# A transformer pair on one core: joined first group, norm factors by token first, weight pieces of one conversion

## Chip, cores and metric

One core of a Trainium2 chip. The metric is the device time of one execution in microseconds (us), the median over runs. One profiled execution by itself gives the views that are quoted here.

## What is computed

256 tokens of width 2048, all in float32, go through two blocks.

The first block: an rms norm, one projection `proj = rmsnorm(h) @ w_in + b_in` cut into q, k, v, gates and convolution inputs, an mLSTM of 4 heads, a short causal convolution, two branch projections merged by sigmoid gates and `w_out`; then a norm, `w_up`, a causal depthwise convolution, `silu(gate) * val`, `w_down`, and a last norm.

The second block has two layers, each `x = x + rms_norm(mixer(rms_norm(x)))`: a gated linear attention (GLA, chunks of 64, 4 heads) and a latent attention (MLA, 16 heads, low-rank queries and keys of width 512 that are normed, rotary halves, softmax, `silu` gates).

The norm that occurs everywhere is

```python
y = x * rsqrt(mean(x * x) + eps) * g
```

where the factor belongs to a token. The kernel multiplies by g before a projection and by the factor R after it.

## The kernel before, in words

Activations lie with features on the 128 partitions and the 256 tokens along the free dimension: `h` has 16 blocks of 128x256 (`KD` = 16). Every projection goes through `dense`. Float32 precision comes from a split of both operands into a high part (fp32r) and the rest: `split` (L425) makes the parts of an activation block with one ScalarE (ACT) and one VectorE (DVE) instruction (L434, L435), and `need` (L301) those of the weights (L312 on ACT, L313 on DVE). For each unit of 128 weight columns, `dense` issues a pair of matmuls: the high weights with 512 moving columns (L359) and the low weights with 256 (L360). The kind "B" (v, gv) has three matmuls with 344 columns (L372 to L374).

`plan` (L46) lists all projections as groups in the order of the run, cuts the stream of weight units into conversions of at most `SUB` = 1040 columns (`subs`, 721 of them), and joins two of these to a piece (`pieces`, 361). A piece is one transfer by SyncE's queue (SP, L299) into one of `RAW` = 3 raw buffers of 2 x 1040 columns. `wunit` (L320) asks for the conversion that is `st["look"]` = `LOOK` = 3 ahead of the one in use; there are `LOOK` + 1 = 4 buffers `hl` for converted pieces. A conversion waits for its transfer and for TensorE to finish with the buffer that it overwrites; a transfer waits for DVE's conversion of the raw buffer's old content.

An accumulator `acc` has two banks for two output blocks, and there are two of them. A group of four blocks takes both: it runs the first half of the input blocks for all four outputs, then the second half for the first two outputs, then for the last two. `evac` (L409) empties an accumulator with one ACT and one DVE instruction, at a priority raised by 150.

The scheduler orders each engine's instructions by priority, which is the order in the program unless raised, with a model of times; on the chip every engine then runs its queue in that order. `tc.issue_after(st["mm"])` keeps a side matmul behind the last matmul of a group.

The start (L538 to L573): nine junk matmuls, then transfers of x blocks (`xload`) and parts of the first pieces in turn, then all 16 splits with three conversions between them. The first norm: squares are summed into `st1` while the four qk groups run (L637 to L646); `mk_R1` (L578) runs after the third. `bc_sum` (L468) sums over features and spreads the sum to all partitions as a row of 256 tokens (R); `col_sum` (L474) puts it in a column with tokens on partitions (Rc), needed by v and gv. `rsqrt` (L463) is a square root on ACT and a reciprocal on DVE. The third norm (`mk_R3`, L866) needs the sums `s3` and `s4` before and after the first block's last norm, and makes Ro, R as rows and Rc as columns.

On GpSimd (POOL), `rope_tables` (L587) computes the rotary angles in one long run of instructions. The bias vb of v comes by three transfers on POOL's queue (L731); DVE adds it when it empties v (L735), first into `ifc`, which TensorE then transposes (L654). In GLA, `gkc` (L892) is the like of ifc; TensorE transposes it at L902.

`out_norm` (L481) runs an output projection and its norm; it lowers the look-ahead to 2 for the last two groups. After GLA, `x3` (L1047) forms the next input block by block: DVE scales y (L1052), POOL adds it to h (L1053), and `split` follows. MLA's low-rank inputs are emptied by `low_rank_in` (L1068); `low_rank_scale` (L1075) makes their row factors; `skc` is a column made from a row by two transposes (L1118 to L1123).

The functions that the change touches stand here:

## Time and profile before

| | |
|---|---|
| median of 3 runs | 2060.18 us (2059.97 to 2061.51) |
| the profiled execution by itself | 2059.47 us |
| its span, first to last instruction | 2057.8 us |
| TensorE matmul busy | 2005.0 us, 97% |
| VectorE busy | 1433.7 us, 70% |
| ScalarE busy | 1153.3 us, 56% |
| GpSimd busy | 392.9 us, 19% |
| DMA | 385.61 MB, mean 187 GB/s |

How to read it: an engine runs its instructions in order, so a stall is found where an instruction has idle time before it, and the releaser named behind it is the instruction that ended the wait. TensorE's idle time is 2057.8 - 2005.0 = 52.8 us in the whole span, the start before its first matmul and the end after its last among it.

### The profile page before, as it was taken

To read this page: it belongs to the slowest core of one execution; us is meant where nothing else is said; L and a number is where in the kernel's file an instruction comes from. 1 tells how busy PE (TensorE), PEld (TensorE's weight loads), DVE (VectorE), ACT (ScalarE), POOL (GpSimd) and SP (SyncE) were. 2 spreads that over 40 slices of the span, in tenths; PEclk is the share of its full clock that TensorE was granted. 3 is DMA by queue.
4 is the path that set the end of the run, shared out by engine and by line. 5 is a ranking of instruction groups with operands and counts; after the bars stand their busy time and mean duration, and the time that the engine had idled before them with its cause. 6 is when DMAs were issued, how large, how long until landed. Compare 5 with 4: busy or idle time off the path is not lost. (4 is left out here: it accounts for less than half of the span.)

```text
span 2057.8 us, 30674 instructions
## 1 busy us (share of the span) xinstructions
PE 2005.0 (97%) x12438; PEld 1849.7 (90%) x12438; DVE 1433.7 (70%) x1758; ACT 1153.3 (56%) x1599; POOL 392.9 (19%) x333
## 2 busy tenths in 40 slices
PE   8799999999999999999999999999999999999997
PEld 7788999999999999999999999989999988989996
DVE  7568776666667888864588876676767558777754
ACT  6454555555556666654466666655666556544453
POOL 8511000010122111100011113321220025112312
PEclk9999999999999999999999999999999999999998
DMA  7443555555555555555555555535545544554343
GB/s 289 155 164 144 204 200 204 191 204 204 205 201 188 205 204 198 198 200 206 203 205 203 197 195 206 205 120 198 180 171 188 201 170 178 194 188 145 109 165 112
DMA packets 55743, 385.61 MB, mean 187 GB/s; under 512 B 6384, under 2 KB 6640, under 8 KB 10544
## 3 DMA queue, kind: packets, MB, share of 16 engines
q1 hardware_dynamic: 55152, 382.91, 51.5%
q8 instruction: 97, 1.59, 0.3%
q0 software_dynamic: 304, 0.73, 0.1%
q14 instruction: 46, 0.38, 0.1%
q10 hardware_dynamic: 144, 0.01, 0.0%
HBM read 381.52 MB, written 2.10 MB: 186 GB/s over the span
## 5 line engine op out<-in xcount | busy, mean ns | idle before, releaser
L313 DVE TENSOR_TENSOR hl<-raw,hl 128x1024 fp32r<-128x1024 f32 (+3 forms) x722 | 941.0, 1311 | 353.3 <-ACT hl L312 352.8
L359 PE MATMUL acc<-xhl,hl 128*128 128x512 f32 x3440 | 1138.1, 384 | 9.5 <-DVE xhl L435 7.8
L312 ACT ACTIVATE hl<-raw 128x1024 fp32r<-128x1024 f32 (+3 forms) x722 | 756.8, 1052 | 395.3 <-PE acc L360 250.5
L360 PE MATMUL acc<-xhl,hl 128*128 128x256 f32 x3440 | 940.9, 274 | 1.6 <-DVE hl L313 1.6
L359 PEld LDWEIGHTS acc<-xhl,hl 128*128 128x128 f32 x3440 | 652.6, 190 | 105.0 <-DVE xhl L435 6.9
L360 PEld LDWEIGHTS acc<-xhl,hl 128*128 128x128 f32 x3440 | 662.7, 193 | 3.3 <-DVE hl L313 2.9
L359 PE MATMUL acc<-ghl,hl 128*128 128x512 f32 x688 | 225.4, 382 | 0.0
L412 ACT ACTIVATE t<-acc 128x512 f32<-128x512 f32 x138 | 82.2, 596 | 192.6 <-PE acc L360 171.8
L360 PE MATMUL acc<-ghl,hl 128*128 128x256 f32 x688 | 187.5, 273 | 0.0
L413 DVE TENSOR_TENSOR u<-acc,t 128x512 f32<-128x512 f32 x138 | 94.9, 688 | 104.3 <-ACT t L412 104.3
L418 POOL TENSOR_TENSOR uR<-u,R 128x512 f32<-128x512 f32 x51 | 69.8, 1369 | 443.3 <-DVE u L413 436.0
L359 PEld LDWEIGHTS acc<-ghl,hl 128*128 128x128 f32 x688 | 130.0, 189 | 18.1
L360 PEld LDWEIGHTS acc<-ghl,hl 128*128 128x128 f32 x688 | 132.1, 192 | 0.0
L456 POOL TENSOR_TENSOR ss<-ss,sq 128x512 f32<-128x512 f32 x41 | 64.9, 1584 | 223.0 <-ACT sq L451 213.6
L374 PE MATMUL acc<-hl,xhl 128*128 128x344 f32 x288 | 90.4, 314 | 1.5 <-DVE hl L313 1.5
L372 PE MATMUL acc<-hl,xhl 128*128 128x344 f32 x288 | 91.0, 316 | 0.0
L373 PE MATMUL acc<-hl,xhl 128*128 128x344 f32 x288 | 90.3, 313 | 0.0
L795 POOL TENSOR_TENSOR m<-u 128x256 f32<-128x256 f32 x16 | 24.9, 1553 | 336.1 <-DVE u L793 336.1
L783 PE MATMUL acc<-hmxc,hl 128*128 128x512 f32 x256 | 84.7, 382 | 0.0
L359 PE MATMUL acc<-mg,hl 128*128 128x512 f32 x256 | 83.9, 382 | 0.0
L831 ACT ACTIVATE cv<-uR,vec 128x256 f32<-128x256 f32 x86 | 46.9, 593 | 57.9 <-POOL uR L418 57.9
L359 PE MATMUL acc<-ohl,hl 128*128 128x512 f32 x224 | 73.7, 383 | 0.0
(515 smaller groups left out, 2490.2 us busy)
## 6 DMA issues: line engine op xcount, KB each, us to landing
raw<-stream SPq DMA_DIRECT2D x330, 1024.0 KB, 4.8
raw<-stream SPq DMA_DIRECT2D x21, 1032.0 KB, 4.8
raw<-stream SPq DMA_DIRECT2D x4, 512.0 KB, 7.2
out<-y SPq DMA_DIRECT2D x8, 256.0 KB, 2.1
h<-xT SPq DMA_DIRECT2D x7, 256.0 KB, 7.2
raw<-stream SPq DMA_DIRECT2D x1, 1028.0 KB, 4.7
raw<-stream SPq DMA_DIRECT2D x1, 1008.0 KB, 4.7
raw<-stream SPq DMA_DIRECT2D x1, 988.0 KB, 6.6
```

What stands on the lines that cost most here:

```text
L312: S.activation(hl[:, 0, x:y_], src, AF.Copy)
L313: V.tensor_tensor(hl[:, 1, x:y_], src, hl[:, 0, x:y_].bitcast(F32), op=ALU.subtract)
L359: PE.matmul(o, lhsT=wh, rhs=both(x), start=(k == 0), stop=False)
L360: mm = PE.matmul(o[:, T:2 * T], lhsT=wl, rhs=part(x, 0), start=False, stop=(k == nk - 1))
L372: PE.matmul(o, lhsT=xh, rhs=both(wh), start=(k == 0), stop=False)
L373: PE.matmul(o, lhsT=xl, rhs=both(wh), start=False, stop=False)
L374: mm = PE.matmul(o, lhsT=xh, rhs=both(wl), start=False, stop=(k == nk - 1))
L412: S.activation(halves(t[:, :nb]), out_of(ps[:, :nb, T:2 * T]), AF.Copy)
L413: V.tensor_tensor(halves(u[:, :nb]), out_of(ps[:, :nb, 0:T]), halves(t[:, :nb]), op=ALU.add)
L418: (eng or V).tensor_tensor(w[:, :nb], u[:, :nb], bc2(R)[:, :nb], op=ALU.mult)
L456: (eng or G).tensor_tensor(self.ss, self.ss, sq, op=ALU.add)
L783: PE.matmul(o, lhsT=wh, rhs=both(x), start=(k == 0), stop=False)
```

## The change

`plan` joins the first two qk groups to one group of four blocks, and a piece is now one conversion. There are four raw buffers of 1040 columns and five converted buffers. The start transfers fewer x blocks ahead of the first pieces, and the splits are made as `dense` asks for them, four blocks ahead (`lazy`). The first norm's factors are made after the fourth qk group; all factors but the second norm's and the heads' are made as columns by token (`col_sum`, `second`) and turned into rows by `to_row`: a diagonal matrix from the column and the identity, and a matmul with ones. The joined group's evacuations, and those of cq, lose the raised priority. vb is transferred by SyncE's queue.

```diff
--- before.py
+++ after.py
@@ -61,7 +61,8 @@
         g.append(dict(name=name, kind=kind, blocks=blocks, k0=k0, nk=nk, n=nk * n, order=order))
 
     W = "w_in"
-    for h in range(4):
+    add("qk", "A", [(W, _blk(o + h * P)) for h in range(2) for o in (0, 512)], 0, KD)
+    for h in (2, 3):
         add("qk", "A", [(W, _blk(h * P)), (W, _blk(512 + h * P))], 0, KD)
     vcols = np.concatenate([_blk(3072, 8), _blk(1024, 1024)])
     for c in range(3):
@@ -128,8 +129,7 @@
         pos += e["n"]
     subs.append(cur)
     pieces, at = [], 0
-    for i in range(0, len(subs), 2):
-        n = sum(subs[i:i + 2])
+    for n in subs:
         pieces.append((at, n))
         at += n
     return g, subs, pieces, at
@@ -247,7 +247,7 @@
     from contextlib import ExitStack
     es = ExitStack()
     pool = lambda **k: es.enter_context(tc.tile_pool(**k))
-    RAW, LOOK, WARM = 3, 3, 9
+    RAW, LOOK, WARM = 4, 4, 9
     cst = pool(name="cst", bufs=1)
     rawp = pool(name="rawp", bufs=RAW)
     hlp = pool(name="hlp", bufs=LOOK + 1)
@@ -287,10 +287,10 @@
     def emit_dma(upto):
         while st["dma"] <= min(upto, len(pieces) - 1):
             p = st["dma"]
-            r = rawp.tile([P, 2 * SUB], F32, tag="raw", name="raw")
+            r = rawp.tile([P, SUB], F32, tag="raw", name="raw")
             raws[p] = r
             st["dma"] += 1
-            if p > 1:
+            if p > 3:
                 piece_dma(p, 0, pieces[p][1])
 
     def piece_dma(p, x, y_):
@@ -301,19 +301,16 @@
     def need(q_):
         while st["sub"] <= min(q_, len(subs) - 1):
             q = st["sub"]
-            p, half = divmod(q, 2)
-            emit_dma(p + RAW - 1)
+            emit_dma(q + RAW - 1)
             n = subs[q]
-            o = subs[q - 1] if half else 0
             hl = hlp.tile([P, 2, SUB], F32R, tag="hl", name="hl")
-            cuts = (0, n) if q else (0, n // 2, n)
+            cuts = (0, n) if q else (0, n // 4, n // 2, n)
             for x, y_ in zip(cuts, cuts[1:]):
-                src = raws[p][:, o + x:o + y_]
+                src = raws[q][:, x:y_]
                 S.activation(hl[:, 0, x:y_], src, AF.Copy)
                 V.tensor_tensor(hl[:, 1, x:y_], src, hl[:, 0, x:y_].bitcast(F32), op=ALU.subtract)
             hls[q] = hl
-            if half == 1:
-                raws.pop(p, None)
+            raws.pop(q, None)
             hls.pop(q - 8, None)
             st["sub"] += 1
 
@@ -406,9 +403,9 @@
     def bc2(r):
         return r[:, None, :].to_broadcast([P, 2, T])
 
-    def evac(ps, nb=2):
+    def evac(ps, nb=2, ahead=150):
         t, u = tt("t"), tt("u")
-        with tc.high_priority(offset=150):
+        with tc.high_priority(offset=ahead):
             S.activation(halves(t[:, :nb]), out_of(ps[:, :nb, T:2 * T]), AF.Copy)
             V.tensor_tensor(halves(u[:, :nb]), out_of(ps[:, :nb, 0:T]), halves(t[:, :nb]), op=ALU.add)
         return u
@@ -478,13 +475,33 @@
                 PE.matmul(ps[:, t:t + 1], lhsT=ss[:, t * P:(t + 1) * P], rhs=ones[:, 0:1], start=True, stop=True)
         return ps[:, 0:2]
 
+    def to_row(dst, c_):
+
+        dg, pr = tt("dg"), sm()
+        for t in range(2):
+            V.tensor_scalar(dg[:, 0, t * P:(t + 1) * P], ident, c_[:, t:t + 1], None, op0=ALU.mult)
+            with tc.issue_after(st["mm"]):
+                PE.matmul(pr[:, t * P:(t + 1) * P], lhsT=ones, rhs=dg[:, 0, t * P:(t + 1) * P], start=True, stop=True)
+        S.activation(dst, pr[:, 0:T], AF.Copy)
+
+    def col_tile(tag):
+        return stp.tile([P, 2], F32, tag=tag, name=tag)
+
+    def second(dst, c_, total, n):
+
+        w = col_tile("cw")
+        V.tensor_tensor(w, total, c_, op=ALU.mult)
+        V.tensor_tensor(w, w, c_, op=ALU.mult)
+        rsqrt(w, w, 1.0 / n)
+        V.tensor_tensor(dst, w, c_, op=ALU.mult)
+
     def out_norm(name, IN, g, y):
 
         st_ = Stat("a")
         parts = []
         warm = stp.tile([P, 1], F32, tag="warm", name="warm")
         for js in TAIL:
-            st["look"] = LOOK if js[0] < 14 else 2
+            st["look"] = LOOK if js[0] < 14 else LOOK - 1
             ps = dense(name, IN)
             if len(js) == 2:
                 u = evac(ps)
@@ -544,32 +561,25 @@
     pw = sm()
     for i in range(WARM):
         PE.matmul(pw[:, 0:P], lhsT=junk[:, 0:P], rhs=junk[:, P:T], start=True, stop=True)
-    emit_dma(1)
+    emit_dma(3)
     xload = lambda x, y_: nc.sync.dma_start(h[:, x:y_], a["xT"][:, x:y_])
-    s0, n0, n1 = subs[0], pieces[0][1], pieces[1][1]
+    s0 = subs[0]
     xload(0, 1)
-    piece_dma(0, 0, s0 // 2)
+    piece_dma(0, 0, s0 // 4)
+    piece_dma(0, s0 // 4, s0 // 2)
     xload(1, 2)
+    piece_dma(0, s0 // 2, s0)
     xload(2, 4)
-    piece_dma(0, s0 // 2, s0)
+    piece_dma(1, 0, subs[1])
     xload(4, 6)
-    piece_dma(0, s0, n0)
+    piece_dma(2, 0, subs[2])
     xload(6, 8)
-    xload(8, 10)
-    piece_dma(1, 0, subs[2])
-    xload(10, 12)
-    xload(12, 14)
-    piece_dma(1, subs[2], n1)
-    xload(14, 16)
-    emit_dma(2)
-    nc.sync.dma_start(con, a["con"])
-    nc.sync.dma_start(vec[:, 16:nvec], a["vec"][:, 16:nvec])
+    piece_dma(3, 0, subs[3])
+    xload(8, 12)
+    xload(12, 16)
     _, X = hl_tiles(2, "xhl")
-    need(0)
-    for k in range(KD):
-        split(X(k), h[:, k], vc("g_mix", k))
-        if k in (2, 6, 10):
-            need(k // 4 + 1)
+    X_ = X
+    X = lazy(X_, lambda k: split(X_(k), h[:, k], vc("g_mix", k)), 4)
     st1 = Stat("a")
 
     R = row_tile("R")
@@ -577,8 +587,8 @@
 
     def mk_R1():
         ss = st1.fold(V)
-        rsqrt(R, bc_sum(ss), 1.0 / D)
         rsqrt(Rc, col_sum(ss), 1.0 / D)
+        to_row(R, Rc)
 
     COS, SIN = row_tile("COS"), row_tile("SIN")
     turn = inv_two_pi()
@@ -634,16 +644,18 @@
         V.tensor_scalar(qk[:, hd, 1], uR[:, 1], vc("bk", hd), float(P) ** -0.5, op0=ALU.add, op1=ALU.mult)
 
     held = []
+    ps = dense("qk", X)
+    nc.sync.dma_start(con, a["con"])
+    nc.sync.dma_start(vec[:, 16:nvec], a["vec"][:, 16:nvec])
+    held += [evac(p_, ahead=0) for p_ in ps]
+    X = X_
+    for hd in (2, 3):
+        for k in range(8 * hd - 16, 8 * hd - 8, 2):
+            st1.add(h[:, k:k + 2], eng=V)
+        held.append(evac(dense("qk", X)))
+    mk_R1()
     for hd in range(4):
-        u = evac(dense("qk", X))
-        held.append(u)
-        for k in ((0, 2, 4), (6, 8, 10), (12, 14), ())[hd]:
-            st1.add(h[:, k:k + 2], eng=V)
-        if hd == 2:
-            mk_R1()
-        if hd >= 2:
-            while held:
-                qk_out(hd + 1 - len(held), held.pop(0))
+        qk_out(hd, held[hd])
     ccol = stp.tile([P, 2, 4], F32, tag="ccol", name="ccol")
     rw = lambda i: rows[0:4, i, :]
 
@@ -728,7 +740,7 @@
 
     for c in range(3):
         vb = tt("vb").rearrange("p a t -> p (a t)")
-        nc.gpsimd.dma_start(vb[:, 0:VB], a["bv"][c:c + 1, :].to_broadcast([P, VB]))
+        nc.sync.dma_start(vb[:, 0:VB], a["bv"][c:c + 1, :].to_broadcast([P, VB]))
         ps = dense("v", X)
         ifc = tt("ifc")
         for t in range(2):
@@ -865,16 +877,12 @@
 
     def mk_R3():
         s3, s4 = st3.fold(), st4.fold()
-        for (ro, r, f) in ((Ro, R, bc_sum), (None, Rc, col_sum)):
-            n = T if f is bc_sum else 2
-            w = tt("w")
-            ro = ro if ro is not None else w[:, 1, 0:n]
-            rsqrt(ro, f(s3), 1.0 / D)
-            t = w[:, 0, 0:n]
-            V.tensor_tensor(t, f(s4), ro, op=ALU.mult)
-            V.tensor_tensor(t, t, ro, op=ALU.mult)
-            rsqrt(t, t, 1.0 / D)
-            V.tensor_tensor(r, t, ro, op=ALU.mult)
+        t3, t4 = col_sum(s3), col_sum(s4)
+        c3 = col_tile("c3")
+        rsqrt(c3, t3, 1.0 / D)
+        second(Rc, c3, t4, D)
+        to_row(R, Rc)
+        to_row(Ro, c3)
 
     gb = big(name="gb")
     gbT = gb[:, 0:2048].rearrange("p (b t) -> p b t", b=8)
@@ -1066,21 +1074,18 @@
     gates = big(F32, (P, KD, T), name="gates")
 
     def low_rank_in(which, s, q, ps):
-        u = evac(ps)
+        u = evac(ps, ahead=150 if which else 0)
         s.add(u)
         for b in range(2):
             i = 2 * q + b
             split(cqkv[:, 4 * which + i], u[:, b], vc(("g_qa", "g_kva")[which], i))
 
-    def low_rank_scale(s, tag):
-        ss = s.fold()
+    def low_rank_scale(s, tag, c6):
+        c_ = col_tile("c" + tag)
+        second(c_, c6, col_sum(s.fold()), 512)
         r = row_tile(tag)
-        w = tt("w")
-        V.tensor_tensor(w[:, 0], R, R, op=ALU.mult)
-        V.tensor_tensor(w[:, 1], bc_sum(ss), w[:, 0], op=ALU.mult)
-        rsqrt(w[:, 1], w[:, 1], 1.0 / 512)
-        V.tensor_tensor(r, w[:, 1], R, op=ALU.mult)
-        return r
+        to_row(r, c_)
+        return r, c_
 
     sa, sb = Stat("a"), Stat(None, gates[:, 14:16])
     ps = dense("cq", X)
@@ -1107,20 +1112,16 @@
     for j in range(8):
         u = evac(dense("mgate", X))
         if j == 0:
-            rsqrt(R, bc_sum(st6.fold()), 1.0 / D)
+            c6 = col_tile("c6")
+            rsqrt(c6, col_sum(st6.fold()), 1.0 / D)
+            to_row(R, c6)
             uR = times_R(ukr, R, 1)
             rope([(kr[0:64, 0], 0, 64), (kr[64:128, 1], 64, 128)], uR[:, 0], (V, V, G, G))
         s = times_R(u, R, eng=G)
         S.activation(gates[:, 2 * j:2 * j + 2], s, AF.Silu)
         if j == 1:
-            sq_ = low_rank_scale(sa, "sq")
-            skv = low_rank_scale(sb, "skv")
-        if j == 2:
-            pc = sm()
-            for t in range(2):
-                PE.transpose(pc[:, t:t + 1], skv[0:1, t * P:(t + 1) * P], con[0:1, C_ID:C_ID + 1])
-            skc = stp.tile([P, 2], F32, tag="Rc", name="skc")
-            V.tensor_copy(skc, pc[:, 0:2])
+            sq_, _ = low_rank_scale(sa, "sq", c6)
+            skv, skc = low_rank_scale(sb, "skv", c6)
 
     _, OX = hl_tiles(2, "ohl")
     XQ = lambda k: cqkv[:, k]
```

## Rows read from the trace of the kernel before

**Rows 1.** The page's first part: busy us, share of the span, instructions.
```profile
PE 2005.0 (97%) x12438; PEld 1849.7 (90%) x12438; DVE 1433.7 (70%) x1758; ACT 1153.3 (56%) x1599; POOL 392.9 (19%) x333
```

**Rows 2.** Waits of TensorE: line, waited for, us in total, times, longest.
```profile
PE sm L654 <- DVE ifc L735: 10.6, 1, 10.6
PE acc L359 <- DVE xhl L435: 7.8, 6, 2.6
PE sm L902 <- DVE gkc L892: 4.7, 1, 4.7
PE acc L372 <- DVE mq L1170: 4.2, 4, 2.5
...
PE acc L374 <- DVE hl L313: 1.5, 1, 1.5
...
PE sm L471 <- DVE ss L460: 1.2, 1, 1.2
```

**Rows 3.** Windows: stretch, its us, busy us per engine, PEclk, DMA share, GB/s.
```profile
75.10:85.36 10.26, 3.76 (x15) 3.44 (x16) 2.71 (x6) 0.77 (x1) 4.34 (x7) 0.50 0.20 52
1355.10:1358.50 3.40, 2.92 (x11) 2.77 (x12) 2.64 (x6) 0.00 (x0) 0.00 (x0) 0.50 0.60 188
13.68:17.09 3.41, 3.41 (x13) 2.96 (x12) 3.41 (x7) 3.41 (x7) 3.16 (x4) 0.50 1.05 424
```

**Rows 4.** Windows: a steady stretch of the up projection.
```profile
900.00:1100.00 200.00, 200.00 (x1224) 183.97 (x1223) 124.08 (x134) 100.63 (x121) 19.19 (x15) 1.00 0.56 202
```

**Rows 5.** Timeline at the ifc stall (start, us, what, idle before); vb's DMA row.
```profile
77.32 0.72 POOL L602 TENSOR_TENSOR COS<-COS,ecv 128x256 f32<-128x256 f32 x1
77.99 1.70 POOL L731 DMA_DIRECT2D vb<-bv  x3
...
81.60 0.37 PE L654 MATMUL sm<-con,ifc 128*4 128x128 f32 x1 [10.61 <-DVE ifc L735]
...
vb<-bv POOLq DMA_DIRECT2D x3, 172.0 KB, 3.5
```

**Rows 6.** Timeline of the third norm's chain, DVE and TensorE.
```profile
1337.17 1.75 DVE L466 RECIPROCAL R<-R 128x256 f32<-128x256 f32 x1 [1.09 <-ACT R L465]
...
1340.38 0.17 DVE L466 RECIPROCAL w<-w 128x2 f32<-128x2 f32 x1
...
1350.75 1.22 DVE L877 TENSOR_TENSOR Rc<-w 128x2 f32<-128x2 f32 x1
...
1355.58 0.38 PE L902 MATMUL sm<-con,gkc 128*16 128x128 f32 x1 [4.67 <-DVE gkc L892]
```

**Rows 7.** The start: timeline of TensorE and ACT; DVE's conversions; the window.
```profile
5.53 0.79 PE L359 MATMUL acc<-xhl,hl 128*128 128x512 f32 x1
...
10.47 1.06 ACT L312 ACTIVATE hl<-raw 128x1024 fp32r<-128x1024 f32 x1 [0.40 <-DMA raw<-stream]
...
22.83 0.60 ACT L412 ACTIVATE t<-acc 128x512 f32<-128x512 f32 x1 [1.83 <-PE acc L360]
...
L313 DVE TENSOR_TENSOR hl<-raw,hl 128x1024 fp32r<-128x1024 f32 (+1 forms) x7 | 8.4, 1218 | 2.9 <-ACT hl L312 2.9
...
4.00:23.00 19.00, 15.97 (x74) 12.94 (x74) 15.53 (x23) 13.38 (x25) 13.78 (x14) 0.91 1.00 381
```

**Rows 8.** Timeline: the third norm's two column sums; an out_norm's diagonal matmuls.
```profile
1335.42 0.95 PE L478 MATMUL sm<-con,ss 128*128 128x1 f32 x8
...
1689.96 0.71 PE L517 MATMUL sm<-dg,con 128*128 128x128 f32 x4 [0.87 <-DVE dg L516]
```

**Rows 9.** DMA issues: KB each, median us from issue to landing.
```profile
raw<-stream SPq DMA_DIRECT2D x330, 1024.0 KB, 4.8
...
raw<-stream SPq DMA_DIRECT2D x4, 512.0 KB, 7.2
out<-y SPq DMA_DIRECT2D x8, 256.0 KB, 2.1
```

**Rows 10.** Timeline of ACT: a conversion in the steady stretch.
```profile
910.31 1.06 ACT L312 ACTIVATE hl<-raw 128x1024 fp32r<-128x1024 f32 x1 [1.56 <-PE acc L360]
```

## The prediction, made before the changed kernel ran

> **What bounds the kernel now.** I read the page first. TensorE is busy for 2005.0 of 2057.8 us [rows 1], so it is the bound almost everywhere, and only three kinds of time can be won: idle time of TensorE, time at its lower clock, and matmuls removed. The second view is TensorE's waits; the six that the change can touch make 30.0 us [rows 2]. The waits of 10.6 and of 4.7 us are single stalls. The third view is the windows around stalls [rows 3]: in the three windows there, of 3.4 to 10.3 us, the granted clock is 0.50, its lower level of 1.2 GHz, and each has TensorE waiting in it or just before it. A busy microsecond there does half a microsecond of work. The fourth view is the timeline at each stall. All the rest is TensorE at its rate: a stretch without idle time, 200 us long, holds 612 pairs of a 512-column and a 256-column matmul, 0.327 us a pair [rows 4]; the change leaves all these pairs in place. A piece of 1024 columns is eight pairs, 2.62 us.
>
> The profiled execution took 2059.47 us by itself (span 2057.8), 0.71 below the median of the runs, 2060.18. The sum is made against 2059.47, and 0.7 is added at the end.
>
> **Bias by SyncE.** The 10.6 us stall: TensorE stands at a transpose (L654) that reads ifc, and DVE computes ifc with the value bias vb, whose three transfers POOL issues at 77.99, straight behind the last instruction of the rope tables (L602) [rows 5]. So the transfer is late because of its queue; it lands 3.5 us after issue. Moved to SyncE's queue, the first vb has ahead of it the weight transfers that are earlier in program order. v starts at the 17th piece; with four raw buffers and five converted ones, the transfers ahead of vb wait for TensorE to finish at most the 15th. So vb is issued before v starts, and v's first group takes five pieces, 13 us, which hides the landing. The three issues lie beside a queue that mostly waits for raw buffers. If a vb has to wait for its tile, only weight transfers stand behind it, covered by the pieces ahead. A short wait for DVE's ifc instruction stays: an estimate of 0.3, twice the 0.17 of a small DVE operation [rows 6]. Idle gain 10.6 - 0.3 = 10.3. Behind the stall 3.76 us of TensorE time run at 0.50 [rows 3]; at full clock that is 1.9. Term: 12.2 us, bounds 10.3 (the clock falls all the same) and 12.5.
>
> **Norm factors by token.** The 4.7 us stall: TensorE stands at L902 for gkc, which needs Rc. DVE makes R and Rc in a chain that starts with a 1.75 us reciprocal of 128x256 at 1337.17 and goes on through row and column operations, with weight conversions between, to Rc at 1350.75 [rows 6]. In the new code only 128x2 operations stand before Rc. The small reciprocal took 0.17 us [rows 6]; about eight such operations, each behind one conversion of 1.22 us [rows 7] at worst, make 11 us. That is done by 1348, while TensorE comes to L902 at 1350.9 (1355.58 less 4.67). Idle gain 4.7 - 0.3 = 4.4; of the 2.92 busy us at half clock behind it [rows 3] 1.4 come back. Term: 5.8, bounds 3.0 (a chain still 2.8 late) and 6.1.
>
> At the other places six broadcast sums go (R of the first norm, two of the third, R6, two low-rank) and six row copies through a diagonal come; both stream 256 columns, so they are equal on TensorE. Three column sums come: the two that stand together now took 0.95 [rows 8], so 1.4 for three. The wait of 1.2 us for DVE's fold at the first norm [rows 2] goes, since the adds now end a group before the sum. The row copy has a chain of its own: DVE diagonal, matmul, ACT copy. Where it stands alone, at an out_norm, its matmul waited 0.87 us [rows 8]; here other matmuls lie between, and only this matmul waits for the diagonal, so I take 0.5 for all six. DVE loses row reciprocals of 1.75 us, which saves nothing where conversions are in time. Term: 1.2 - 0.5 - 1.4 = -0.7; bounds -5.4 (six waits of 0.87) and 1.2.
>
> **Joined first group.** The first pair starts at 5.53, the first group's evacuation at 22.83 [rows 7]. Its 32 pairs need 10.5 us, so 6.8 are lost, the most to be won. From 4 to 23 us DVE is busy for 15.5 of 19 us, and transfers run at 381 GB/s throughout [rows 7]. The second piece's conversion waits for its transfer until 10.47 [rows 7]; up to it six blocks of x (0.79 MB) and 1.05 MB of weights were issued. In the new order four blocks of x (0.52 MB) stand before the same weights: 0.26 MB less, 0.7 us at that rate, so 9.8. Conversion then takes 1.06 (ACT) and up to 1.5 (DVE): 12.4. The 24 pairs from there end at 20.3, 2.5 before 22.83. In the old stretch 3.41 us run at half clock [rows 3], 1.7 of loss; if that comes again, 0.8 are won. Term: 1.7, between the two. Bounds: 6.8, and -3.6: the joined group holds both accumulators and its evacuation has lost its priority, so the next group can wait for an evacuation (0.60 on ACT [rows 7], the like on DVE) behind one conversion (1.06 and 1.22). I don't take that, since the first accumulator is complete 16 pairs, 5.2 us, before it is needed. The later con and vec transfers have 40 us until the first norm.
>
> **Pieces and the fifth converted buffer.** The memory is the same: 2080 raw columns go, 2080 converted ones come. Away from the start TensorE waits 1.5 us for a conversion (at L374) [rows 2]. The look-ahead grows from three pieces, 7.9 us, to four, 10.5: term 1.5, bounds 0 and 1.5. Before x3's projection TensorE waits 7.8 us for splits [rows 2]; DVE makes conversions between them. One more is done ahead now: term 1.2 (one DVE conversion [rows 7]), bounds 0 and 7.8. The 4.2 us of mq waits [rows 2] have DVE's rope work behind them: 0, bounds 0 and 4.2.
>
> The price of halving: 721 transfers of 0.5 MB for 361, mostly of 1 MB. In the steady stretch the 16 DMA engines are busy 0.56 at 202 GB/s [rows 4], and at the start they moved 424 [rows 3]. A half piece isn't in the steady trace: 0.25 MB to DRAM lands in 2.1 us, 1 MB in 4.8, the crowded 0.5 MB of the start in 7.2 [rows 9]; I take 3.0, on the line between the first two. A raw buffer comes free four pieces before its next content is converted, 10.5 us, above all of these. Term 0.
>
> The Trainium skill, DMA: Bandwidth & Descriptors, section Bandwidth, wants at least 1 MiB a transfer for three quarters of the peak, which speaks against this edit; no run here shows the efficiency of half a MB. By it the second rival below would gain weight.
>
> **Sum.** 12.2 + 5.8 - 0.7 + 1.7 + 1.5 + 1.2 = 21.7. 2059.5 - 21.7 + 0.7 = 2038.5, say **2038 us**.
>
> **Rivals.**
> - *vb stays late.* SyncE's in-order queue holds it behind a weight transfer, or its tile isn't free, past v's end. For it: conversions wait for TensorE [rows 10], and the transfers of SyncE for conversions. Against it: the order worked out above. The 12.2 are lost: 2050.
> - *Half pieces starve the stream (slower).* Place: the whole weight stream. If the transfers went one at a time, each piece would take 3.0 against 2.62 us of TensorE: 721 x 0.38 = 274 us, 2310. It decides from the point where a piece lands later than 10.5 us after its issue. Against it: DMA engines at 0.56, and several transfers in flight.
> - *More slack where there was strain.* With DVE freed, the start and x3 win most of their losses, 5 of 6.8 and 5 of 7.8: 3.3 + 3.8 more, 2031. For it: DVE is nearly full at the start [rows 7]. Against it: supply limits the start too, and POOL's adds stand in x3's chain.
> - *The fifth buffer does nothing.* ACT's conversions wait for TensorE already [rows 10], so a deeper look-ahead fills and helps nowhere: 2.7 lost, 2041.
>
> **How the numbers follow.** Forecast or idle buffer, 2034 to 2046: 0.70. vb late: 0.10. More slack: 0.15. Slower: 0.03. The rest, 0.02, is no change by several small losses. The range takes in the vb rival above and goes past the third rival below: 2028 to 2050. A measurement of this kernel can tell about 0.2%, 4 us, from no change: faster 0.95, same 0.02, slower 0.03.
>
> **What would show it.** TensorE's wait at the transpose of ifc under 1 us, with vb issued by SyncE before the first v matmul; the wait for gkc under 1 us; a clock of 1.0 at those two places; the 32nd pair done near 20 to 21; no wait for a weight transfer after 20 us. The forecast falls if vb lands after v's first group, if the next group waits for the joined group's evacuation, if the diagonals show waits of 0.9 each, or if conversions begin to wait for transfers.

## The result, and the profile after

| | before | after |
|---|---|---|
| median of 4 runs each, on one chip | 2060.65 us (2059.97 to 2061.51) | 2044.47 us (2042.18 to 2046.44) |
| ratio, with its 95% interval | | 0.9921 (0.9904 to 0.9938) |
| the profiled execution by itself | 2059.47 us | 2046.44 us |
| its span | 2057.8 us | 2044.7 us |

The kernel became 16.2 us faster; 2038 was forecast, with a range from 2028 to 2050. The profiled execution of after is the slowest of its four. A second profile of the same kernel (last experiment) took 2044.32, and where the two differ both are given.

The first part of the page after, against [rows 1]:

```profile
PE 2005.5 (98%) x12460; PEld 1850.3 (90%) x12460; DVE 1432.9 (70%) x1764; ACT 1156.9 (57%) x1605; POOL 391.1 (19%) x330
```

TensorE is as busy as before. The span is 13.1 us shorter, and this is idle time: 52.8 before, 2044.7 - 2005.5 = 39.2 now. TensorE's waits after, with the columns of [rows 2]:

```profile
PE acc L356 <- DVE xhl L432: 6.1, 5, 2.6
PE acc L369 <- DVE mq L1171: 4.1, 4, 2.5
PE acc L357 <- DVE hl L311: 4.0, 2, 3.0
...
PE acc L356 <- ACT hl L310: 3.4, 2, 2.9
...
PE sm L910 <- DVE gkc L900: 1.1, 2, 0.8
PE sm L484 <- DVE dg L482: 0.8, 1, 0.8
PE sm L989 <- POOL A L692: 0.7, 1, 0.7
```

The 10.6 us for ifc are gone from the list, gkc fell from 4.7 to 1.1, and the 1.5 at the GLA conversion is gone too. In their place two waits of some 3 us stand for weight conversions (L356 on ACT, L357 on DVE). Both lie in the first 25 us. In the second profile they are 1.6 and 1.4 us.

**The bias** in the timeline after: its first transfer, and DVE's ifc, which TensorE no longer waits for.

```profile
62.75 0.42 SPq L743 DMA_DIRECT2D vb<-bv  x1
...
73.93 0.23 DVE L747 SCALAR_TENSOR_TENSOR ifc<-acc,Rc,vb 128x8 f32<-128x8 f32 x1 [0.53 <-PE acc L371]
```

SyncE issues it 11 us before ifc needs it, POOL issued it at 77.99 [rows 5]. ifc now waits only for TensorE's own accumulator.

**The third norm** after, timeline of DVE and then of TensorE:

```profile
1331.52 0.15 DVE L496 TENSOR_TENSOR Rc<-cw,c 128x2 f32<-128x2 f32 x1
...
1341.99 0.22 DVE L900 TENSOR_SCALAR gkc<-acc,Rc 128x16 f32<-128x16 f32 x1
1342.13 2.15 DVE L311 TENSOR_TENSOR hl<-raw,hl 128x1032 fp32r<-128x1032 f32 x1
1344.21 0.22 DVE L900 TENSOR_SCALAR gkc<-acc,Rc 128x16 f32<-128x16 f32 x1
```

```profile
1342.27 0.28 PE L910 MATMUL sm<-con,gkc 128*16 128x128 f32 x1 [0.30 <-DVE gkc L900]
...
1344.49 0.28 PE L910 MATMUL sm<-con,gkc 128*16 128x128 f32 x1 [0.78 <-DVE gkc L900]
```

Rc is there 10 us ahead of its first use; before it came at 1350.75, with TensorE waiting [rows 6]. What is left are two short waits, the second because a weight conversion of 2.15 us stands between the two gkc in DVE's queue.

**The start** after, timeline of ACT, then of DVE, then of TensorE, with [rows 7] as the counterpart:

```profile
7.42 0.51 ACT L431 ACTIVATE xhl<-h,vec 128x256 fp32r<-128x256 f32 x1 [2.46 <-DMA h<-xT]
...
8.90 0.63 ACT L310 ACTIVATE hl<-raw 128x512 fp32r<-128x512 f32 x1 [0.46 <-DMA raw<-stream]
...
10.87 1.06 ACT L310 ACTIVATE hl<-raw 128x1024 fp32r<-128x1024 f32 x1 [0.38 <-DMA raw<-stream]
...
16.06 3.30 ACT L431 ACTIVATE xhl<-h,vec 128x256 fp32r<-128x256 f32 x8 [0.20 <-DMA h<-xT]
```

```profile
18.41 4.63 DVE L432 SCALAR_TENSOR_TENSOR xhl<-h,vec,xhl 128x256 fp32r<-128x256 f32 x8
22.96 5.75 DVE L311 TENSOR_TENSOR hl<-raw,hl 128x1024 fp32r<-128x1024 f32 x4
```

```profile
5.11 0.53 PE L356 MATMUL acc<-xhl,hl 128*128 128x512 f32 x1
...
9.59 0.70 PE L356 MATMUL acc<-xhl,hl 128*128 128x512 f32 x2 [2.86 <-ACT hl L310]
...
21.39 0.38 PE L356 MATMUL acc<-xhl,hl 128*128 128x512 f32 x1
24.76 0.38 PE L357 MATMUL acc<-xhl,hl 128*128 128x256 f32 x1 [2.98 <-DVE hl L311]
```

The last of these waits in the second profile:

```profile
24.20 0.38 PE L357 MATMUL acc<-xhl,hl 128*128 128x256 f32 x1 [1.36 <-DVE hl L311]
```

Two things went wrong here. First, supply: the second x block and the third cut of the first piece came late, so TensorE waits 2.86 us after its first four pairs (1.63 in the second profile). Second, order: the eight splits of x blocks 8 to 15 stand in one run of 4.63 us on DVE ahead of the conversion that TensorE needs at 21.8. It comes at 24.76. The four other kernels with this start (experiments 1, 3, 4 and 6) wait 2.84 to 2.99 us at the same place. The windows of the first microseconds, before and then after (columns as in [rows 3]):

```profile
4.00:6.00 2.00, 1.93 (x8) 1.44 (x7) 0.98 (x2) 1.29 (x4) 0.00 (x0) 1.00 0.88 292
```

```profile
4.00:6.00 2.00, 2.00 (x12) 1.95 (x12) 1.30 (x3) 0.81 (x2) 0.00 (x0) 1.00 1.04 153
...
25.74:29.15 3.41, 3.41 (x13) 2.87 (x12) 2.97 (x3) 0.00 (x0) 3.24 (x3) 0.50 0.82 264
...
1360.35:1367.18 6.83, 6.83 (x21) 5.26 (x20) 1.94 (x4) 6.24 (x8) 0.00 (x0) 0.50 0.01 2
1677.80:1688.00 10.20, 8.37 (x25) 6.89 (x26) 9.36 (x13) 6.78 (x12) 4.93 (x3) 0.50 0.28 100
```

The DMA engines were fully busy from 4 to 6 us and delivered 153 GB/s, against 292 before (131 at a share of 0.94 in the second profile). The other three windows are stretches at 1.2 GHz, the lower level: one behind the wait of 2.98, one behind the third norm, one at x3. The second profile has the last two as well; its stretch at the start lasts 6.8 us from 10.0 on.

**Where the time went, stage by stage.** Both kernels empty accumulators 138 times in the same order, so the start of the k-th emptying by ACT is a mark that can be subtracted. Five marks before, then the same five after:

```profile
56.65 0.60 ACT L412 ACTIVATE t<-acc 128x512 f32<-128x512 f32 x1 [0.82 <-PE acc L360]
122.52 0.60 ACT L412 ACTIVATE t<-acc 128x512 f32<-128x512 f32 x1 [1.56 <-PE acc L360]
732.15 0.60 ACT L412 ACTIVATE t<-acc 128x512 f32<-128x512 f32 x1 [1.56 <-PE acc L360]
1388.94 0.58 ACT L412 ACTIVATE t<-acc 128x512 f32<-128x512 f32 x1
1718.67 0.60 ACT L412 ACTIVATE t<-acc 128x512 f32<-128x512 f32 x1 [1.79 <-PE acc L360]
```

```profile
57.96 0.60 ACT L409 ACTIVATE t<-acc 128x512 f32<-128x512 f32 x1 [1.55 <-PE acc L357]
113.47 0.60 ACT L409 ACTIVATE t<-acc 128x512 f32<-128x512 f32 x1 [1.56 <-PE acc L357]
723.11 0.60 ACT L409 ACTIVATE t<-acc 128x512 f32<-128x512 f32 x1 [1.56 <-PE acc L357]
1375.55 0.57 ACT L409 ACTIVATE t<-acc 128x512 f32<-128x512 f32 x1
1706.05 0.58 ACT L409 ACTIVATE t<-acc 128x512 f32<-128x512 f32 x1
```

At the last qk group after is 1.3 us behind (in the second profile 0.9 ahead). At the first emptying behind v it leads by 122.52 - 113.47 = 9.05, and 610 us later by 9.04: the whole steady stream, with halved pieces and the fifth buffer, changes nothing at all. The third norm makes 13.39 of it (+4.3). At the first emptying behind x3 the lead is 12.62: it shrinks there.

The same subtraction for every kernel of this study: how much the lead over before grows (us) in each stage, worked out from such rows of the single profiled executions. "start" ends behind v at 122.52 of before, "third norm" at 1388.94, "GLA" at 1443.93, "A" (TensorE's wait for POOL's A lies in it) at 1677.17, "x3" at 1718.67, "cq" at 1732.92, "low rank" at 1792.20, "end" at 2031.67. From 122.52 to 1324.27, ahead of the third norm, every kernel's lead is constant within 0.1, so this stretch has no column of its own.

```
kernel                      start  third   GLA      A     x3     cq   low    end    sum
                                   norm                              rank
after                        9.05   4.34   1.08  -0.19  -1.66   0.96  -1.08   0.13  12.63
after, second profile       11.41   4.63   0.80  -0.37  -1.72   0.96  -1.07   0.11  14.75
exp. 1  vb by POOL           0.44   3.79   1.63  -1.24  -1.64   0.96  -1.08   1.65   4.51
exp. 2  before + vb by SP   11.84  -1.16   0.52   0.01  -0.58  -0.01   0.00   0.00  10.62
exp. 3  third norm old      11.78   0.22   2.11  -0.87  -1.53   0.95  -1.07   0.20  11.79
exp. 4  all norms old       11.80   0.11   2.11  -3.29  -1.70   0.96   0.00   1.80  11.79
exp. 5  before + pieces     -1.76  -0.02   3.20  -1.44  -0.83   0.00   0.00   1.82   0.97
exp. 6  look-ahead 3        11.79   4.75  -0.01   0.00  -1.68   0.96  -1.07   1.55  16.29
exp. 7  joined group undone 11.02   4.96   2.66  -0.19  -0.46   0.96  -1.07   0.35  18.23
exp. 8  x late              13.18   4.95   2.11  -0.43  -1.54   0.96  -1.07   0.10  18.26
exp. 9  x late again        12.67   4.95   2.12  -0.19  -1.57   0.96  -1.07   0.13  18.00
exp. 10 x late, halves      12.07   4.95   2.11  -0.32  -1.54   0.96  -1.07   0.12  17.28
exp. 11 x late, ACT's queue 13.41   4.96   3.20  -0.30  -1.63   0.96  -1.07   1.82  21.35
```

The columns "GLA" and "end" also differ between kernels with the same code there, in steps of 1 to 2 us, and the granted clock tells why. In "end" it is one stretch of 3.4 us at half clock, worth 1.7: experiments 1, 4, 5, 6 and 11 have none near 1840, the others one.

### The profile page after: what moved, and what is told of

Its sections match the earlier page's. It is cut to its first block, busy times and chain, and to the rows that moved or that the text cites. A ratio compares the mean times of both kernels' runs of the same rounds, so it can differ in the third digit from the quotient of the medians.

```text
span 2044.7 us, 32020 instructions
## 1 busy us (share of the span) xinstructions
PE 2005.5 (98%) x12460; PEld 1850.3 (90%) x12460; DVE 1432.9 (70%) x1764; ACT 1156.9 (57%) x1605; POOL 391.1 (19%) x330
## 5 line engine op out<-in xcount | busy, mean ns | idle before, releaser
L311 DVE TENSOR_TENSOR hl<-raw,hl 128x1024 fp32r<-128x1024 f32 (+2 forms) x723 | 948.5, 1319 | 349.1 <-ACT hl L310 348.2
L356 PE MATMUL acc<-xhl,hl 128*128 128x512 f32 x3440 | 1140.5, 385 | 9.5 <-DVE xhl L432 6.1
L310 ACT ACTIVATE hl<-raw 128x1024 fp32r<-128x1024 f32 (+2 forms) x723 | 756.9, 1050 | 386.3 <-PE acc L357 231.9
L357 PE MATMUL acc<-xhl,hl 128*128 128x256 f32 x3440 | 941.8, 274 | 4.1 <-DVE hl L311 4.0
L356 PEld LDWEIGHTS acc<-xhl,hl 128*128 128x128 f32 x3440 | 653.8, 190 | 105.4 <-issue 5.1
L357 PEld LDWEIGHTS acc<-xhl,hl 128*128 128x128 f32 x3440 | 664.0, 193 | 5.6 <-DVE hl L311 5.3
L356 PE MATMUL acc<-ghl,hl 128*128 128x512 f32 x688 | 225.4, 382 | 0.0
L357 PE MATMUL acc<-ghl,hl 128*128 128x256 f32 x688 | 187.5, 273 | 0.0
L356 PEld LDWEIGHTS acc<-ghl,hl 128*128 128x128 f32 x688 | 130.0, 189 | 18.0
L357 PEld LDWEIGHTS acc<-ghl,hl 128*128 128x128 f32 x688 | 132.1, 192 | 0.0
L356 PE MATMUL acc<-mg,hl 128*128 128x512 f32 x256 | 83.9, 382 | 0.0
L356 PE MATMUL acc<-ohl,hl 128*128 128x512 f32 x224 | 73.7, 383 | 0.0
```

Source lines behind the costliest of these rows:

```text
L310: S.activation(hl[:, 0, x:y_], src, AF.Copy)
L311: V.tensor_tensor(hl[:, 1, x:y_], src, hl[:, 0, x:y_].bitcast(F32), op=ALU.subtract)
L356: PE.matmul(o, lhsT=wh, rhs=both(x), start=(k == 0), stop=False)
L357: mm = PE.matmul(o[:, T:2 * T], lhsT=wl, rhs=part(x, 0), start=False, stop=(k == nk - 1))
```

## The experiments

Each kernel ran on one chip beside the kernel before, whose median was 2060.4 there in experiments 1 to 3, 5 to 8 and 10, and 2061.5 in experiments 4, 9 and 11. All ratios are against these; a difference to after is one to its first median, 2044.47, unless another is named.

**1. vb by POOL again, all else as after.** One term of the sum taken out.

```diff
-        nc.sync.dma_start(vb[:, 0:VB], a["bv"][c:c + 1, :].to_broadcast([P, VB]))
+        nc.gpsimd.dma_start(vb[:, 0:VB], a["bv"][c:c + 1, :].to_broadcast([P, VB]))
```

> The changed kernel with one edit undone: vb is transferred by POOL's queue again. If the bias transfer is the main gain (about 12 of 16 us), TensorE stands at the transpose of ifc until the rope tables end and vb lands, as before at 81.6 us; it now arrives there at about 73, so 8 to 9 us of waiting come back, and a window at the lower clock behind it: about 2055 us, a ratio to the kernel before of 0.997. If the gain comes from elsewhere and vb was hidden, the time stays at 2044.

Measured: 2055.79 us, ratio 0.9976 (0.9966 to 0.9986), 11.3 above after. TensorE's waits of this kernel:

```profile
PE sm L666 <- DVE ifc L747: 7.9, 1, 7.9
```

The stall is back. It is 7.9 and not 10.6 because TensorE arrives later, at 73.3 instead of 71.0, while POOL issues vb at 77.42, near the 77.99 of before: the end of the rope tables doesn't depend on TensorE.

**2. Only vb by SyncE, all else as before.** The same edit from the other side (the line of experiment 1 reversed, in the old kernel).

> The kernel before with one edit of the change alone: vb by SyncE's queue. If its worth doesn't depend on the other edits, the wait at the transpose of ifc falls from 10.6 us to under 0.5 and the lower clock behind it goes: 12.2 us by the prediction, 2048 us. If the gain needs the column factors (Rc early), the wait shrinks only in part: 2052 or more.

Measured: 2048.69 us, ratio 0.9943 (0.9926 to 0.9960), 11.7 below before. The stall for ifc is not among the waits. One line is worth 11.3 to 11.7 us, seven tenths of the whole gain.

**3. The third norm as before, all else as after.**

```diff
-        t3, t4 = col_sum(s3), col_sum(s4)
-        c3 = col_tile("c3")
-        rsqrt(c3, t3, 1.0 / D)
-        second(Rc, c3, t4, D)
-        to_row(R, Rc)
-        to_row(Ro, c3)
+        for (ro, r, f) in ((Ro, R, bc_sum), (None, Rc, col_sum)):
...
```

> The changed kernel with the third norm's factors as rows and columns of the old code, all else kept. If the chain of row operations made the 4.7 us wait for gkc, the wait comes back and with it a window at the lower clock: about 2049 us. If the wait had gone by the fifth converted buffer or another order on DVE, the time stays at 2044.

Measured: 2048.71 us, ratio 0.9942 (0.9927 to 0.9957), 4.2 above after. The timeline of TensorE in this kernel, and the windows of its two stretches at half clock:

```profile
1343.81 0.38 PE L914 MATMUL sm<-con,gkc 128*16 128x128 f32 x1 [4.68 <-DVE gkc L904]
```

```profile
1343.30:1346.70 3.40, 2.89 (x11) 2.74 (x12) 2.67 (x6) 0.00 (x0) 0.00 (x0) 0.50 0.57 161
1363.80:1367.20 3.40, 3.40 (x13) 2.93 (x12) 0.81 (x2) 3.37 (x4) 0.00 (x0) 0.50 0.02 5
```

With the stall, two stretches of 3.4 us run at half clock, 6.8 in sum. Without it, after has one stretch of 6.83 (the window above). So the change won back the idle time and not the clock, in that profile. In the other profiles with the new third norm the half-clock time there is 6.8 twice, 3.4 three times (experiments 8 to 10) and none three times (6, 7, 11). With the pieces of after, the columns "third norm" and "GLA" add up to 5.4 where it is 6.8, 7.1 where it is 3.4, and 7.6 and 8.2 where there is none, against 2.3 and 2.2 for the old norm with the same pieces (experiments 3 and 4).

**4. All norm factors as before.** As experiment 3, with the first norm, the sixth (st6) and the two low-rank norms put back too.

```diff
+        rsqrt(R, bc_sum(ss), 1.0 / D)
         rsqrt(Rc, col_sum(ss), 1.0 / D)
-        to_row(R, Rc)
...
-            c6 = col_tile("c6")
-            rsqrt(c6, col_sum(st6.fold()), 1.0 / D)
-            to_row(R, c6)
+            rsqrt(R, bc_sum(st6.fold()), 1.0 / D)
...
```

> The changed kernel with all norm factors made as before (first norm, third norm, MLA's input norm and low-rank factors by broadcast sums, row reciprocals and two row transposes), all else kept. The run with the third norm alone undone took 2048.7. By the prediction's term of -0.7 for the other places, this one is at 2048 (under 2048.7 by less than the spread). If the other places are worth 2 us or more of what the single edits don't account for, it is at 2051 or more.

Measured: 2049.21 us, ratio 0.9942 (0.9928 to 0.9956), the ratio of experiment 3. The other norm places are worth nothing that can be measured.

**5. The pieces alone, all else as before.** Four raw and five converted buffers, a transfer per conversion, vb and norms as they were.

```diff
-    for i in range(0, len(subs), 2):
-        n = sum(subs[i:i + 2])
+    for n in subs:
...
-    RAW, LOOK, WARM = 3, 3, 9
+    RAW, LOOK, WARM = 4, 4, 9
```

> The kernel before with the piece edit alone: pieces of one conversion, four raw buffers, five converted ones, the same order of x blocks and weights at the start. If half pieces slow the supply of the first 10 us (in the run with the old start the first group's evacuation came at 24.2 instead of 22.8 us), the first evacuation comes near 24 us, the waits for conversions by GLA shrink, and the time is 2060 to 2062: no gain. If the edit is worth its forecast 2.7 us, 2057.

Measured: 2059.94 us, ratio 0.9998 (0.9989 to 1.0007): nothing. The second emptying in this kernel's timeline stands at

```profile
39.11 0.60 ACT L408 ACTIVATE t<-acc 128x512 f32<-128x512 f32 x1 [0.32 <-PE acc L356]
```

and at 33.31 in the kernel before, so this kernel is 5.8 us late there: con and vec stand ahead of the fifth piece in SyncE's queue, and there are four raw buffers of one conversion where there were three of two. Which of the two makes it was not isolated. Behind v only 1.76 us of it are left (column "start"), because TensorE arrives at the stall for ifc later and waits 5.6 us there instead of 10.6. A loss ahead of a wait with a fixed end is hidden in part; with vb early it would show.

The GLA conversion wait did fall here, from 1.5 to 0.3, and the column "GLA" shows a gain of 3.2 (with one stretch of 3.4 at half clock fewer than before). What is late next takes part of it back: TensorE's wait for POOL's A, a little later, rises from 0.5 to 1.9 (column "A": -1.44), and x3 loses 0.83. "end" gains 1.82 by a stretch at half clock that is missing. From v to the end this profile gains 2.7 us, with 13.7 us at half clock there as in before. So its total of nothing is a start that loses 1.8 and a remainder that gains 2.7.

**6. Look-ahead 3 with four converted and six raw buffers, all else as after.**

```diff
-    RAW, LOOK, WARM = 4, 4, 9
+    RAW, LOOK, WARM = 6, 3, 9
...
-            emit_dma(q + RAW - 1)
+            emit_dma(q + (RAW - 1 if q > 7 else 3))
```

> The changed kernel with six raw buffers of one conversion and four converted ones (look-ahead 3) in the same memory, so that only the fifth converted buffer is undone. If it is worth its term of 1.5 to 2.7 us, TensorE's waits for a conversion near the GLA decay (1.5 us) and the larger x3 waits come back: 2046 to 2047. If a conversion buffer more does nothing in this kernel, 2044 within the spread; if fewer raw buffers cost, under 2043.

Measured: 2044.67 us, ratio 0.9922 (0.9908 to 0.9937), the time of after. Its waits hold the old line again:

```profile
PE acc L371 <- DVE hl L311: 1.5, 1, 1.5
```

The column "GLA" is -0.01 here, so in its place the fifth buffer is worth something, and in the total it can't be seen. The test isn't clean: two more raw buffers came with it, the first emptying came 2.7 us earlier (29.07 against 31.76, and 30.23 in the second profile of after), and this profile has half-clock time only at x3 and at the very end. Experiment 11 has its half-clock time at the same two places, and behind v its code differs from this kernel's only in these buffers and the look-ahead that goes with them. From v to the mark at 2031.67 its lead grows by 7.9 us, here by 4.5. TensorE's waits for conversions behind v account for most of the difference: 2.9 us here, the 1.5 above and 1.4 shortly before it, against one of 0.3 there. Two rows of this kernel's timeline, and the wait in experiment 11:

```profile
1368.60 0.38 PE L357 MATMUL acc<-xhl,hl 128*128 128x256 f32 x1 [0.78 <-DVE hl L311]
...
1371.91 0.38 PE L357 MATMUL acc<-xhl,hl 128*128 128x256 f32 x1 [0.43 <-DVE hl L311]
```

```profile
PE acc L373 <- DVE hl L313: 0.3, 1, 0.3
```

The totals may hide this. The four executions here were granted 0.9930 of the clock on average, the nine of after 0.9918; an estimate from these is 0.0012 x 2044 = 2.5 us, if TensorE was busy in all of that time. Whether the shorter look-ahead itself changes the clock isn't shown.

**7. The joined first group undone, all else as after.**

```diff
-    add("qk", "A", [(W, _blk(o + h * P)) for h in range(2) for o in (0, 512)], 0, KD)
-    for h in (2, 3):
+    for h in range(4):
...
-    X = lazy(X_, lambda k: split(X_(k), h[:, k], vc("g_mix", k)), 4)
+    need(0)
+    for k in range(KD):
+        split(X(k), h[:, k], vc("g_mix", k))
...
```

> The changed kernel with the joined group undone: four qk groups of two blocks, x blocks and pieces in the old order of transfers, all splits ahead, normal priority of these evacuations; pieces of one conversion, five converted buffers, factors by token after the fourth qk group and vb on SyncE stay. If the joined start loses about 3.4 us, the fourth qk evacuation starts near 54 to 55 us instead of 57.96 and the time is about 2041. If the joined start wins as forecast (1.7) and the late fourth evacuation comes from something else, the evacuation starts at 59 or later and the time is 2046 or more.

Measured: 2041.8 us, ratio 0.9908 (0.9893 to 0.9923), 2.7 below after. Without this edit the change would have been no slower, and by the medians faster. Its profile doesn't put that in the start: the lead behind v is 11.02, within the 9.05 to 11.80 of the four profiles with the joined start, vb early and four raw buffers (after twice, experiments 3 and 4). Its advantage stands in "GLA" and "x3", where the code is the same and the half-clock time is less. The four executions were granted 0.9928 of the clock on average, against 0.9918 for after, an estimate of 2 us (0.0010 x 2044). So what of the 2.7 belongs to the joined group stays open, between 0 and 2.7 lost. A gain of 1.7 is in neither reading.

**8. x late: the same joined group, x blocks 10 to 15 transferred two at a time behind pieces 4 to 6.** It takes the run of eight splits apart, since a split is made when its block is expected.

```diff
             if p > 3:
                 piece_dma(p, 0, pieces[p][1])
+                if p < 7:
+                    xload(2 * p + 2, 2 * p + 4)
...
-    xload(8, 12)
-    xload(12, 16)
+    xload(8, 10)
```

> The changed kernel with the last eight x blocks transferred two at a time between the pieces 3 to 7, so that the splits of blocks 8 to 15 no longer stand in one run ahead of the fifth piece's conversion on ACT and DVE. If that order causes the 2.98 us wait at 24.8 us, the wait goes, the lower clock behind it (1.7 us) too, and the time is 2040 to 2041. If transfers are what limits that stretch, the wait only moves to another piece or x block and the time stays within 1 us of 2044.

Measured: 2041.84 us, ratio 0.9910 (0.9895 to 0.9925), 2.6 below after. DVE's timeline in this kernel:

```profile
17.91 1.00 DVE L434 SCALAR_TENSOR_TENSOR xhl<-h,vec,xhl 128x256 fp32r<-128x256 f32 x2
18.84 1.42 DVE L313 TENSOR_TENSOR hl<-raw,hl 128x1024 fp32r<-128x1024 f32 x1
20.18 1.01 DVE L434 SCALAR_TENSOR_TENSOR xhl<-h,vec,xhl 128x256 fp32r<-128x256 f32 x2
```

Two splits and a conversion alternate, the wait of 2.98 is gone, and the first emptying comes at 27.63 instead of 31.76. The waits for splits and conversions that are left between 20 and 28 us are 0.34 at most here, and 0.20 at most in experiments 9 and 10. So the run of eight splits was the cause of that wait.

**9. x late once more, and after once more, beside each other.**

> The kernel with the last x blocks late a second time, with more rounds and beside the changed kernel on one chip. If its gain of 2.6 us over the changed kernel is real, it stays 2 to 3 us below it here; if it was the spread of four runs, under 1 us.

> The changed kernel itself a second time, on the same chip as the three others, as their reference: 2044 to 2045.

Measured: x late 2041.04, ratio 0.9904 (0.9890 to 0.9918); after 2044.32, ratio 0.9918 (0.9905 to 0.9932). x late is faster than after by 3.3 on this chip, and was by 2.6 in experiment 8: it beats both kernels. The two profiles agree with that, by "start": 13.18 and 12.67 against 9.05 and 11.41. The clock doesn't make it: 0.9920 on average over the eight executions of x late, 0.9918 over the nine of after. Experiment 7, without the joined group, came to the same time as x late, so a joined group with x late isn't shown to be better than none.

**10. x late, with the first piece in halves instead of a half and two quarters.**

```diff
-            cuts = (0, n) if q else (0, n // 4, n // 2, n)
+            cuts = (0, n) if q else (0, n // 2, n)
```

> The kernel with the last x blocks late (the one that ran at 2041.8), with the first piece cut in two halves instead of two quarters and a half. If small cuts (1 KB per partition) cost supply at the start, the ACT wait for the third cut goes and the time is about 1 us lower, 2041. If the first matmuls wait longer for a half than for a quarter, 2042 to 2043.

Measured: 2043.09 us, ratio 0.9915 (0.9900 to 0.9929). Against x late (experiment 8) this is 1.2 more, with intervals that overlap: no gain from larger cuts, and more can't be said. Without the quarters the stretch from 4 to 6 us delivers 116 GB/s.

**11. x late, with x blocks 1 to 3 by ACT's queue.** It asks whether the low supply of the first microseconds is the DMA engines' or the one queue's.

```diff
-    xload(1, 2)
+    nc.scalar.dma_start(h[:, 1:2], a["xT"][:, 1:2])
...
-    xload(2, 4)
+    nc.scalar.dma_start(h[:, 2:4], a["xT"][:, 2:4])
```

> The kernel with the last x blocks late, and blocks 1 to 3 of x transferred by ACT's queue instead of SyncE's. If the shortage from 4 to 8 us (120 to 190 GB/s there against 292 in the kernel before) comes from one queue's order, the ACT waits of 1.8 and 0.8 us there shrink and the time is 2040 to 2041. If the DMA engines themselves are slow in those microseconds, it stays within 1 us of the kernel with the last x blocks late.

Measured: 2040.58 us, ratio 0.9901 (0.9888 to 0.9915). The windows of this kernel:

```profile
4.00:6.00 2.00, 1.99 (x8) 1.45 (x7) 0.60 (x2) 0.42 (x1) 0.00 (x0) 1.00 1.00 312
...
1330.00:1380.00 50.00, 48.92 (x307) 45.28 (x306) 38.16 (x49) 30.00 (x36) 15.04 (x10) 1.00 0.48 148
```

From 4 to 6 us the same DMA engines deliver 312 GB/s (x late alone: 138 in its second profile), so 138 was not the most they can do there. From 2 to 4 us they deliver less, 158 against 230, and from 2 to 10 us it is 297 against 266. The total is within 0.5 us of x late, and that with more clock (0.9938 on average against 0.9920), so no gain is shown: the first cuts of weights now come later (5.00 and 6.60 on ACT, 3.74 and 4.36 in x late's second profile), TensorE needs both, and it waits 1.36 us for a split at 25.9.

## Why the prediction was right, and where it was not

**Bias by SyncE: right.** 12.2 forecast, 11.3 and 11.7 measured from two sides. The issue stands before v, the wait is gone, and no stretch at 1.2 GHz stands there any more. The landing took 5.1 us (median) where 3.5 was read from [rows 5], and the pieces ahead cover it.

**Third norm: the mechanism right, the size off.** 5.8 forecast, 4.2 measured by medians. The idle part was nearly right: 4.7 - 1.1 = 3.6 against 4.4; I had not seen that a conversion can stand between the two gkc, which costs the second 0.78. What failed is the 1.4 us of clock "come back". Before has two half-clock stretches of 3.4 there, the first in [rows 3], the second at 1375.6. In both profiles of after the first is gone and the second twice as long. So the sign "a clock of 1.0 at those two places" holds, and the time was lost 16 to 18 us later. Where it isn't lost, the gain is about what was forecast: 8.2 - 2.2 = 6.0 in experiment 11, 5.4 - 2.2 = 3.2 in after.

**Other norm places: right.** -0.7 forecast, nothing measurable by medians (experiments 3 and 4 have one ratio). The column "low rank" shows -1.1 in every kernel with the new low-rank factors and 0.0 in the kernels without. Of the diagonals only the first norm's shows in the list of waits, with 0.8, and the wait for the fold is gone. The gain of 0.96 under "cq" was not forecast; it comes with neither vb nor the pieces and stays with the old norms. It also stays with the joined group undone (experiment 7) and with look-ahead 3 (experiment 6). What the change leaves in that stage is the raised priority that the evacuations of cq lost; that this makes the 0.96 is a conclusion by elimination, and no run tested it alone.

**Joined first group: wrong.** 1.7 forecast; 0 to -2.7 measured. The step that failed is the estimate of the second piece's conversion at 9.8 and of all that follows "at that rate". It stands at 10.87 (10.32 in the second profile), about where it was before, 10.47, though 0.26 MB less was ahead of it: the 381 GB/s were an average of 19 us, and the new start delivers 153 from 4 to 6 us. The 32nd pair was then done at about 21.6 (forecast 20.3, sign 20 to 21), still earlier than before. The second step that failed isn't in the prediction at all. I counted DVE's load at the start, but not the order in its queue: the eight splits that become ready together with the last two x transfers go ahead of a due conversion. That costs 2.98 and the 3.41 at half clock behind it, 4.7 in all in that profile; in the second profile the wait is 1.36. Experiment 8 shows it by taking it away. The evacuation wait that I had feared for the negative bound did not occur.

**Fifth buffer: found in its place, not in the total, and left open.** 1.5 and 1.2 forecast, nothing measured in the total (experiments 5 and 6), as the rival "the fifth buffer does nothing" has it. The single profiles speak against that rival. At equal half-clock time the gain behind v is 2.7 in experiment 5 and 3.4 between experiments 6 and 11, near the 2.7 forecast. In the totals it can lie hidden, behind a start that loses 1.8 in the one and behind more clock in the other. These are one profile each, and no total confirms them. In experiments 3 and 4, with as much half-clock time as before, "GLA" gains 2.1. What the sum left out is what is late next: POOL's A takes back 0.9 in experiment 3 (3.3 in experiment 4, where one more stretch at half clock lies there). At x3, where the 1.2 was to be won, TensorE's wait fell by 1.7 (7.8 to 6.1) and the lead shrank by 1.7 all the same, because the half-clock time there is 10.2 us in after and 3.4 in before. It is 10.2 in all other profiles but experiment 7's (6.8), with or without each edit, so no edit can be blamed for it. Before was profiled once, and its other executions may have it as well: the 34 of them beside the experiments were granted 0.9891 of the clock on average, the profiled one 0.990.

**Halved pieces in the steady stream: right.** The price was 0, and the lead is 9.05 and 9.04 at marks 610 us apart. The issues and a steady window after:

```profile
raw<-stream SPq DMA_DIRECT2D x668, 512.0 KB, 3.8
...
vb<-bv SPq DMA_DIRECT2D x3, 172.0 KB, 5.1
```

```profile
900.00:1100.00 200.00, 200.00 (x1223) 183.91 (x1222) 127.78 (x140) 101.50 (x123) 19.14 (x15) 1.00 0.61 201
```

A half piece lands in 3.8 us (3.0 assumed, 10.5 are allowed). The 16 DMA engines are now busy 0.61 for 201 GB/s, before 0.56 for 202 [rows 4]. The Trainium skill, DMA: Bandwidth & Descriptors, section Bandwidth, asks for transfers of at least 1 MiB for three quarters of the peak; the larger busy share for the same bytes agrees in direction, and the time shows that it doesn't matter at this demand. In the first microseconds supply did fall, but the size of a transfer doesn't explain it. Experiment 5 has the transfers of before there, in the same sizes (halves, [rows 9]) and order, and still delivered 233 GB/s from 4 to 6 us against 292, with the second half of the first piece converted at 9.61 instead of 8.20. What made the difference was not isolated.

**The balance.** By medians of single edits: 11.5 + 4.2 + 0 + 0, less 0 to 2.7, makes 13.0 to 15.7 of the 16.2 measured. The rest is within the spread of the medians and of the half-clock time, and the fifth buffer's gain behind v has room in it; no run tells these apart. The forecast was 22 (21.7 and the rounding). The miss of 6 lies in small terms: 1.7 at the start, where nothing or a loss came, 1.5 + 1.2 that no total shows, and the clock at the third norm. The time still lies inside the range, 5.5 below its upper end, because the one large term, the bias, came as forecast.

## What to carry to other kernels

Here a transfer issued from GpSimd's queue came as late as the work ahead of it (77.99 us, against 62.75 from SyncE's): look first for small loads behind long runs of instructions, and move them to a queue that mostly waits for buffers (one line, 11.5 us). Book a removed wait only after naming what is late next, and book clock only when the stretch after it has been followed too. Before calling a term of 2 or 3 us nothing, compare the granted clocks of the executions and the profile stage by stage. In a start-up phase count bytes per microsecond and the order in each engine's queue; eight splits that became ready together ran together here and held up a conversion, and spreading the transfers that they waited for (x late) interleaved them.

## What the runs showed of the hardware that was not expected

TensorE ran at 1.2 GHz from 1360.35 to 1367.18 though it was busy in all 6.83 us of that window and in the microseconds ahead of it: ahead of it and into it run 16 matmuls with 16 input rows each (L920 in the timeline, from 1357.10 to 1362.5), and from 1351 to there no wait is shown. In experiment 11 the clock is 1.00 from 1330 to 1380, around the same 16 matmuls (the window above). So they alone don't decide it; what does was not tried.

The DMA engines can show as fully busy (1.04) and deliver 153 GB/s, while the same stretch of another order delivers 312 at a share of 1.00. In the slow case one queue holds small cuts of weights and x blocks in turn; in the fast one two x transfers come from a second queue. The quarter cuts alone are not the reason, since experiment 10 has none and delivered 116. Which of the transfers held the others up was not isolated.
